# Feed-forward products by one level of Strassen's identity, the second product taken one Strassen product at a time

## The chip, the cores and the metric

The kernel runs on one core of a Trainium2 chip. The metric is the device time of one execution in microseconds (us). The kernel before takes 3463.45 us (median of three runs, 3463.38 to 3473.92). The engines of the core are named as in the profile: PE is the matrix engine (TensorE), DVE VectorE, ACT ScalarE, POOL GpSimd, and SP is the engine whose queue issues every DMA of this kernel.

## The reference, cut to what matters

One post-norm block over 2048 tokens of width 1024: a mixer of two head groups (a state-space group and an RWKV-7 group), an output projection, a layer norm, and then a feed-forward layer with an inner width of 4096 and a last layer norm. Only the feed-forward layer is touched.

```python
D_MODEL = 1024; SEQ = 2048; D_FF = 4 * D_MODEL
def sq_relu_mlp(h, w_fc, w_proj):
    return jnp.square(jax.nn.relu(h @ w_fc)) @ w_proj
...
h = layer_norm(ALPHA * h + mix, ln1_g[l], ln1_b[l])
h = layer_norm(ALPHA * h + sq_relu_mlp(h, w_fc[l], w_proj[l]), ln2_g[l], ln2_b[l])
```

All tensors are float32. The two products are 2048 x 1024 x 4096 ("up") and 2048 x 4096 x 1024 ("down").

## The kernel before, in words

Three phases follow one another: `phase_in` (layer norm, input projection), `phase_rwkv` (both head groups, with the output projection woven in as the pieces of a generator `k.fill`), and `phase_mlp` (the last pieces of `k.fill`, then the feed-forward layer). The tile framework orders the instructions of each engine by a timeline of its own; each engine then works off its list strictly in order, and waits where an operand or a buffer is not ready.

Every matrix product is made in three matmuls. An operand x is split into a high part that the matrix engine's float32r format holds and the rest, `hi` and `lo` (a cast on ACT, a subtraction on DVE or POOL), and the product is hi·hi + lo·hi + hi·lo. One matmul has a 128x128 stationary operand and a 128x512 moving one, and adds into one PSUM bank (128x512 float32).

`phase_mlp` takes the tokens in two blocks of 1024 (`blocks`: the eight middle token tiles first, since they leave the mixer first). For a block the transposed activations stand split in SBUF (`k.hh`, `k.hl`: eight transposes per token tile in PE, line 234, an ACT cast, line 235, a DVE subtraction, line 236). A loop over 16 groups (`NG`) of two 128-wide slices of the inner layer then does, for each slice, `weights` (two 512 KB loads, two casts, two subtractions, lines 1337 to 1349), `up` (2 x 24 matmuls, lines 1360 to 1362, and per 512 tokens a relu, a square, a cast and a subtraction, lines 1364 to 1367), and for the group before it `down` (lines 1380 to 1382, 12 matmuls per 128 tokens x 512 columns, added to an SBUF accumulator by DVE, line 1386). So up and down alternate through the whole phase and nothing goes back to DRAM. `down` of the last group is 24 matmuls per token tile and ends with the layer norm (`ln_apply`) and the store of that tile. `ln_apply` does its two passes over the row in DVE (lines 1306, 1308), or, with `spread`, one in ACT (line 1297) and two in POOL (line 1304).

PSUM has eight banks: `k.ps` has 4 (up, and the output projection's rest), `k.ps2` 4 (down, transposes).

## Time and profile before

| | |
|---|---|
| median of three runs | 3463.45 us |
| time of the profiled execution | 3468.34 us |
| its span, first to last instruction | 3466.6 us |
| mean granted clock of PE over the span | 0.931 |
| PE busy / DVE / ACT / POOL | 91% / 57% / 36% / 31% |
| feed-forward, first up matmul to last down matmul begun | 2033.07 to 3452.22 us |
| matmuls of the feed-forward | 3072 up and 3072 down |

A row of the groups reads: line, engine, operation, output<-inputs, shapes, count, then busy time, mean of one in ns, and the idle time of the engine just before, with what ended it. A row of the timeline reads: start, duration, engine, line, operation, and in brackets the idle time before with its releaser. A row of the windows gives, for a stretch of time, each engine's busy time and instruction count, PE's granted clock, the mean busy share of the 16 DMA engines and what they moved. Matmuls are pipelined: one is shown as busy for some 390 ns, while the next begins sooner.

### The profile page before, as it was taken

The page shows a single profiled execution, that of the slowest core. Times are in us where ns is not written, and L with a number is a line of the kernel's source. Part 1 is how long each engine was busy: PE and PEld are TensorE (multiplying, and loading weights), DVE is VectorE, ACT ScalarE, POOL GpSimd, SP SyncE. Part 2 cuts the span into 40 slices and gives each one's busy share as a digit, 9 for nine tenths or more (in the row PEclk, how much of TensorE's full clock was granted, in tenths as well). Part 3 has the DMA queues.
Part 4 walks back from the last instruction along what each step waited for, and adds up shares of the span by engine and source line. Part 5 has one row for each costly group of instructions (what it writes and reads, how often), then busy time and mean ns, then how long its engine had stood idle before and what let it go on. Part 6 is the DMA issues. An engine that isn't in the chain of part 4 may idle for free.

```text
span 3466.6 us, 62908 instructions
## 1 busy us (share of the span) xinstructions
PE 3166.2 (91%) x24551; PEld 2528.8 (73%) x24551; DVE 1971.3 (57%) x3722; ACT 1238.0 (36%) x2574; POOL 1058.1 (31%) x1742
## 2 busy tenths in 40 slices
PE   5879999988876798999889799999999999999998
PEld 4767867766665576777667578888888788888886
DVE  7798456777674555555766554444444654444446
ACT  3556323433335445455656431222122212222221
POOL 0352134444554333335565551111111111111113
PEclk9989999999985889886988899999999999999999
DMA  5345356776777566667665552111111331111111
GB/s 209 131 161 178 120 150 182 217 217 191 216 220 194 152 160 169 156 155 192 172 168 156 154 185 96 46 48 49 49 46 46 104 109 49 49 49 49 49 49 61
DMA packets 630137, 446.70 MB, mean 129 GB/s; under 512 B 193456, under 2 KB 553552, under 8 KB 629840
## 3 DMA queue, kind: packets, MB, share of 16 engines
q1 hardware_dynamic: 629840, 442.69, 43.7%
q8 instruction: 193, 3.16, 0.4%
q14 instruction: 104, 0.85, 0.1%
HBM read 295.43 MB, written 147.14 MB: 128 GB/s over the span
## 4 chain that ended last, share of the span: by engine, by line
PE 57%; DMA 15%; DVE 11%; issue 4%; POOL 4%; ACT 2%; SPq 2%; POOLq 0%; DVEq 0%; ACTq 0%
PE ps L1360 7%; PE ps L1362 7%; PE ps L1361 7%; PE ps L1382 6%; PE ps L1380 6%; PE ps L1381 6%; DMA R<-rows 2%; PE psg L266 2%; PE psg L267 2%; PE psg L268 2%; PE psg L826 2%; DMA la<-ad 2%; DMA ad<-at 2%; PE ch L1138 2%; DMA nd<-ln 1%
## 5 line engine op out<-in xcount | busy, mean ns | idle before, releaser
L1386 DVE TENSOR_TENSOR acc<-acc,ps 128x512 f32<-128x512 f32 x464 | 318.2, 687 | 445.5 <-PE ps L1382 443.2
L1367 POOL TENSOR_TENSOR ul<-r,uh 128x512 fp32r<-128x512 f32 x128 | 171.4, 1340 | 1186.9 <-ACT uh L1366 1186.9
L1362 PE MATMUL ps<-hl,fh 128*128 128x512 f32 x1024 | 401.8, 392 | 0.0
L1361 PE MATMUL ps<-hh,fl 128*128 128x512 f32 x1024 | 401.2, 392 | 0.0
L1360 PE MATMUL ps<-hh,fh 128*128 128x512 f32 x1024 | 397.7, 393 | 3.4 <-DVE h L831 3.1
L1382 PE MATMUL ps<-ph,ul 128*128 128x512 f32 x1008 | 393.3, 390 | 0.0
L1381 PE MATMUL ps<-pl,uh 128*128 128x512 f32 x1008 | 393.0, 390 | 0.0
L1380 PE MATMUL ps<-ph,uh 128*128 128x512 f32 x1008 | 392.8, 390 | 0.0
L266 PE MATMUL psg<-hh,wh 128*128 128x512 f32 x864 | 356.5, 413 | 9.9 <-ACT u L285 9.1
L267 PE MATMUL psg<-hh,wl 128*128 128x512 f32 x864 | 354.4, 410 | 0.0
L268 PE MATMUL psg<-hl,wh 128*128 128x512 f32 x864 | 352.1, 408 | 1.4 <-DVE hl L236 1.4
L1348 ACT CAST ph<-wraw 128x1024 fp32r<-128x1024 f32 x63 | 63.3, 1050 | 533.8 <-PE ps L1382 528.2
L1360 PEld LDWEIGHTS ps<-hh,fh 128*128 128x128 f32 x1024 | 192.2, 188 | 46.4 <-issue 3.5
L1361 PEld LDWEIGHTS ps<-hh,fl 128*128 128x128 f32 x1024 | 192.3, 188 | 42.7
L1362 PEld LDWEIGHTS ps<-hl,fh 128*128 128x128 f32 x1024 | 192.2, 188 | 42.8
L1382 PEld LDWEIGHTS ps<-ph,ul 128*128 128x128 f32 x1008 | 189.4, 188 | 40.7
L1381 PEld LDWEIGHTS ps<-pl,uh 128*128 128x128 f32 x1008 | 189.2, 188 | 40.8
L1380 PEld LDWEIGHTS ps<-ph,uh 128*128 128x128 f32 x1008 | 189.2, 188 | 40.7
L266 PEld LDWEIGHTS psg<-hh,wh 128*128 128x128 f32 x864 | 169.2, 196 | 49.5 <-ACT u L285 10.3
L1053 POOL TENSOR_TENSOR ltmp<-ln,la 128x30 f32<-128x30 f32 (+10 forms) x480 | 121.6, 254 | 248.7 <-DMA la<-ad 218.5
L268 PEld LDWEIGHTS psg<-hl,wh 128*128 128x128 f32 x864 | 168.2, 195 | 39.2 <-issue 3.0
L267 PEld LDWEIGHTS psg<-hh,wl 128*128 128x128 f32 x864 | 169.1, 196 | 35.7 <-issue 2.3
(291 smaller groups left out, 6148.5 us busy)
## 6 DMA issues: line engine op xcount, KB each, us to landing
h<-hD SPq DMA_DIRECT2D x64, 512.0 KB, 3.6
wraw<-in_w_fc_dram SPq DMA_DIRECT2D x64, 512.0 KB, 4.0
wraw<-in_w_proj_dram SPq DMA_DIRECT2D x64, 512.0 KB, 4.3
rk<-rk SPq DMA_DIRECT2D x64, 384.0 KB, 4.7
eD<-et SPq DMA_DIRECT2D x32, 514.0 KB, 2.7
E<-eD SPq DMA_DIRECT2D x64, 257.0 KB, 4.7
xs<-xg SPq DMA_DIRECT2D x64, 256.0 KB, 4.1
R<-rows SPq DMA_DIRECT2D x64, 256.0 KB, 4.4
```

What stands on the lines that cost most here:

```text
L266: nc.tensor.matmul(pt, wh[:, c], hh[:, c], start=(c == 0), stop=False)
L267: nc.tensor.matmul(pt, wl[:, c], hh[:, c], start=False, stop=False)
L268: nc.tensor.matmul(pt, wh[:, c], hl[:, c], start=False, stop=(c == KC - 1))
L1053: eng.tensor_tensor(tv, ln[:, 0:m, r:r + 1].broadcast_to([P, m, w]), la[:, r:r + 1, r + 1:16].broadcast_to([P, m, w]), ALU.mult)
L1360: nc.tensor.matmul(pt, wh[:, c], k.hh[:, c, ns], start=(c == 0), stop=False)
L1361: nc.tensor.matmul(pt, wl[:, c], k.hh[:, c, ns], start=False, stop=False)
L1362: nc.tensor.matmul(pt, wh[:, c], k.hl[:, c, ns], start=False, stop=(c == KC - 1))
L1367: nc.gpsimd.tensor_tensor(ul[:, ns], r, uh[:, ns], ALU.subtract)
L1380: nc.tensor.matmul(pt, uh[:, ts], ph[:, hs], start=(i == 0), stop=False)
L1381: nc.tensor.matmul(pt, uh[:, ts], pl[:, hs], start=False, stop=False)
L1382: nc.tensor.matmul(pt, ul[:, ts], ph[:, hs], start=False, stop=(i == len(ops) - 1))
L1386: nc.vector.tensor_tensor(acc[j][:, hs], acc[j][:, hs], pt, ALU.add)
```

## The change

Both products go by one level of Strassen's identity (in Winograd's form): each operand is cut into 2 x 2 quarters, seven products of sums of quarters replace eight of quarters.

- **Up.** A step is a token block (1024) and a pair of 128-wide slices (16 pairs, `NP`). Each of the seven products has 12 matmuls into a bank of 512 tokens; products 2 and 3 add into the banks of 1 and 5. Sums of the weight quarters are made by POOL (`sums_a`, 4 operations per step), those of the activations once per block (`hprep`, `sums_b`: on DVE for the first block, on POOL, through DRAM `hT`, for the second). Seven splits of weight sums per step (ACT cast, DVE subtraction). The sums that give the four quarters of the inner activations are made from the banks (`post`: one copy in ACT, five additions in DVE), then relu and square in ACT.
- **Between.** The inner activations do not stay in SBUF. DVE makes the seven left operands of down from their quarters (`sums_a`, 4 operations per step), unsplit, and seven stores per step put them into DRAM (`uD`). The right operands of down are made from `w_proj` in 16 of the 32 steps (`pprep`: 4 loads, 4 POOL sums, 7 stores to `pD`).
- **Down.** It starts after the last step of up. Per block it takes one product after the other (`DOWN`), each over all eight groups of the inner layer; the four 128-token tiles of a product stand in four banks. A step (block, product, group) loads 512 KB of `uD` and 512 KB of `pD`, splits both (two casts in ACT, one subtraction in DVE, one in POOL), three steps ahead, and has 24 matmuls. After a product's eighth group `take` adds the four banks to the right quarters of `y` (the residual, loaded and scaled by ACT at the block's first product); the last two products end with the layer norm and the store.
- **Banks and buffers.** `k.ps` has 6 banks, `k.ps2` 2. The weight tiles `wa`, `wh`, `wl` and the scratch `sc` have one buffer each; the down operands four.

The diff's core:

```diff
+ORDER = (1, 6, 7, 5, 2, 4, 3)
+DOWN = (1, 6, 7, 5, 2, 3, 4)
+def sums_a(eng, a, new):
+    for i in (5, 6, 3):
+        a[i] = new(i)
+    eng.tensor_tensor(a[5], a[7], a[4], ALU.add)
+    eng.tensor_tensor(a[6], a[5], a[1], ALU.subtract)
+    eng.tensor_tensor(a[7], a[1], a[7], ALU.subtract)
+    eng.tensor_tensor(a[3], a[2], a[6], ALU.subtract)
...
+        def hprep(b, i):
+            s = {}
+            for t, slots in ((blocks[b][i], (1, 2)), (blocks[b][4 + i], (7, 3))):
+                h = xp.tile([P, D], F32, name="h", bufs=2)
+                nc.sync.dma_start(h, k.hD[t])
+                for q in range(2):
...
+                    s[slots[q]] = scratch(slots[q])
+                    nc.scalar.copy(s[slots[q]], pt.rearrange("p j t -> p (j t)"))
+            sums_b(nc.gpsimd if b else nc.vector, s, scratch)
+            ts = slice(P * i, P * i + P)
+            for j in ORDER:
+                x = s[j].rearrange("p (c t) -> p c t", c=4)
+                if b:
+                    nc.sync.dma_start(hD[j][:, :, ts], x)
+                else:
+                    split(hh[j][:, :, ts], hl[j][:, :, ts], x)
...
+                mm = [(x[:, n], y[:, n]) for n in range(4) for x, y in ((hi, hh[i]), (lo, hh[i]), (hi, hl[i]))]
+                for n, (x, y) in enumerate(mm):
+                    nc.tensor.matmul(pt, x, y, start=(n == 0 and i not in (2, 3)), stop=(n == 11 and i not in (1, 5)), skip_group_check=True)
+                post(i, pt)
+                after(i)
+                between(i)
+            sums_a(nc.vector, c, lambda i: wp.tile([P, 512], F32, name=f"ua{i}"))
+            for i in ORDER:
+                nc.sync.dma_start(uD[b][q // 2][:, i - 1, q % 2], c[i])
...
+            for src, eng, names in ((uD[b][g], nc.vector, ("uh", "ul")), (pD[g], nc.gpsimd, ("ph", "pl"))):
+                hi, lo = (wk.tile([P, 2, 512], F32R, name=n) for n in names)
+                x = lo.bitcast(F32)
+                nc.sync.dma_start(x, src[:, i - 1])
+                nc.scalar.copy(hi, x)
+                eng.tensor_tensor(lo, x, hi, ALU.subtract)
...
+            for j in range(4):
+                ts = slice(P * j, P * j + P)
+                mm = [(x[:, r, ts], z[:, r]) for r in range(2) for x, z in ((uh, ph), (uh, pl), (ul, ph))]
+                for s, (x, z) in enumerate(mm):
+                    nc.tensor.matmul(banks[j], x, z, start=(g == 0 and s == 0), stop=(g == NG - 1 and s == 5))
+                if g == NG - 1:
+                    take(b, i, j, banks[j])
...
-        k.ps = pool("psumo", 4)
-        k.ps2 = pool("psumo2", 4)
+        k.ps = pool("psumo", 6)
+        k.ps2 = pool("psumo2", 2)
```

The order that the framework makes of it, at three places. In the rows a tile's name is followed by a number of its buffer; `cst` is the identity, `h` a token tile, `woh`, `yh` and the like belong to the output projection, and a wait names the engine or the DMA queue slot that it is for.

**Where up begins, PE.** Before, the last matmul of the output projection is followed by the first of up:

```order
L826 MATMUL ps_24135<-wol_17121,yh_24055 128x512
L826 MATMUL ps_24135<-woh_17120,yl_24057 128x512
L1360 MATMUL ps_24213<-hh_23763,fh_23770 128x512 [waits DMAHW3_49,DMAHW4_49,DMAHW2_49,DMAHW5_49,DMAHW0_49,DVE_49]
L1361 MATMUL ps_24213<-hh_23763,fl_23772 128x512
L1362 MATMUL ps_24213<-hl_23764,fh_23770 128x512
```

Now (L1381 are the transposes of `hprep`, L1495 the matmuls of up, `hh1` and `wh1` the high parts for product 1, `hh6` and `wh6` for product 6):

```order
L826 MATMUL ps_24301<-woh_17120,yl_24239 128x512
L1381 MATMUL ps2_24003<-cst_60,h_24001 128x128 [waits DMAHW0_49,Activation_49]
L1381 MATMUL ps2_24019<-cst_60,h_24017 128x128 [waits DMAHW2_49,Activation_49]
L1381 MATMUL ps2_24111<-cst_60,h_24109 128x128 [waits DMAHW3_49,Activation_49]
L1381 MATMUL ps2_24127<-cst_60,h_24125 128x128 [waits DMAHW4_49,Activation_49]
L1381 MATMUL ps2_24717<-cst_60,h_24715 128x128 [waits DMAHW0_49,Activation_49]
L1495 MATMUL ps_24381<-hh1_23801,wh1_24338 128x512 [waits DVE_49,Activation_49]
L1495 MATMUL ps_24400<-hh6_23803,wh6_24342 128x512 [waits DVE_49,Activation_49]
L1495 MATMUL ps_24381<-hh1_23801,wl1_24339 128x512 [waits DVE_49]
```

The transposes of the third and fourth pair of token tiles of the first block have moved behind the whole output projection, and the second matmul of up belongs to product 6 and waits for that product's weights.

**The first weights, SP and then POOL, now** (`sc` are the scratch tiles that `hprep` uses too, so a load into one waits until DVE has made the last split out of it; L1304 is the layer norm of the last token tile):

```order
L1436 DMA sc1_24217<-in_w_fc_dram 128x4x128 [waits DVE_49]
L1376 DMA h_25284<-hD1_83 128x1024 [waits DMAHW0_49,PE_49]
L1436 DMA sc2_24223<-in_w_fc_dram 128x4x128 [waits DVE_49,Activation_49]
L1436 DMA sc7_24219<-in_w_fc_dram 128x4x128 [waits DVE_49]
L1436 DMA sc4_24221<-in_w_fc_dram 128x4x128 [waits DMAHW6_49,DVE_49]
L836 DMA hD15_97<-h_24232 128x1024 [waits Activation_49,Pool_49]
```

```order
L1330 TENSOR_TENSOR sc5_24225<-sc7_24219,sc4_24221 128x512 [waits DMAHW6_49,DMAHW5_49,DVE_49]
L1304 TENSOR_TENSOR h_24232<-h_24232,b1_17620 128x512 [waits Pool_49]
L1304 TENSOR_TENSOR h_24232<-h_24232,rsb_17622 128x256 [waits Pool_49]
L1304 TENSOR_TENSOR h_24232<-h_24232,rsb_17624 128x256
L1331 TENSOR_TENSOR sc6_24226<-sc5_24225,sc1_24217 128x512 [waits DMAHW2_49,DVE_49,Pool_49]
L1332 TENSOR_TENSOR sc7_24219<-sc1_24217,sc7_24219 128x512 [waits DVE_49]
```

The sum `sc6` that product 6 needs stands behind `sc5` and three operations of a layer norm.

**Where down begins, SP now** (`ua1`, `ua2` and `ua4` are operands that the last step of up stores, `ul` and `pl` the tiles that the loads of down fill, `y` the residual):

```order
L1501 DMA uD1_7_23775<-ua1_30206 128x512 [waits DMAHW2_49,Activation_49]
L1501 DMA uD1_7_23775<-ua2_30222 128x512 [waits DMAHW3_49,Activation_49]
L1539 DMA ul_30265<-uD0_0_23760 128x1024 [waits DMAHW4_49,PE_49]
L1539 DMA pl_30270<-pD0_23776 128x1024 [waits DMAHW5_49,PE_49]
L1539 DMA ul_30275<-uD0_1_23761 128x1024 [waits DMAHW6_49]
```

and, four steps of loads later, the residual of both blocks, eight token tiles ahead of the loads of step 5 and seven ahead of those of step 6:

```order
L1539 DMA ul_30361<-uD0_4_23764 128x1024 [waits DMAHW1_49,DVE_49,PE_49]
L1315 DMA row_g_30294<-in_ln2_g_dram 128x1024 [waits DMAHW2_49]
L1552 DMA y_30298<-hD4_86 128x1024 [waits DMAHW4_49]
L1552 DMA y_30319<-hD11_93 128x1024 [waits DMAHW3_49]
L1539 DMA ul_30395<-uD0_5_23765 128x1024 [waits DMAHW4_49,DVE_49,PE_49]
L1539 DMA pl_30400<-pD5_23781 128x1024 [waits DMAHW5_49,Pool_49]
L1552 DMA y_32414<-hD0_82 128x1024 [waits DMAHW6_49]
L1552 DMA y_32432<-hD14_96 128x1024 [waits DMAHW4_49]
L1539 DMA ul_30429<-uD0_6_23766 128x1024 [waits DMAHW5_49,DVE_49,PE_49]
```

Before, loads of `w_fc` and `w_proj` alternate through the whole phase; now the first loads of down stand behind a store that waits for the last step of up.

More of the change, by code (lines that the diff above doesn't have):

```diff
@@ L1402, in phase_mlp, with wtile, wraw @@
                     break
+        def wtile(i):
+            return wp.tile([P, 512], F32, name=f"wa{i}")
+        def wraw(q, new=wtile):
+            a = {}
+            for i, hf, f in ((1, 0, 0), (7, 0, 1), (4, 1, 1), (2, 1, 0)):
+                a[i] = new(i)
+                c0 = P * (2 * q + f)
+                nc.sync.dma_start(a[i].rearrange("p (c m) -> p c m", c=4),
+                                  I["w_fc"][512 * hf:512 * hf + 512, c0:c0 + P].rearrange("(c p) m -> p c m", p=P))
+            sums_a(nc.gpsimd, a, new)
+            return a
@@ L1403, in phase_mlp @@
+        a = wraw(0, scratch)
         for _ in k.fill:
             pass
-        cp = ctx.enter_context(tc.tile_pool(name="mlp_c", bufs=1))
-        wk = ctx.enter_context(tc.tile_pool(name="mlp_w", bufs=2))
-        rows = load_rows(k, cp, ("ln2_g", "ln2_b"))
-        for bi, toks in enumerate(blocks):
-            acc = []
-            prev = None
-            for gi in range(NG):
-                ops = [up(first.pop() if first else weights(G * gi + i, bi and G * gi + i == DFF // P - 1)) for i in range(G)]
-                if bi == 0 and gi == NG - 1:
-                    operands()
-                    for j, t in enumerate(blocks[1]):
-                        transpose_split(k, load(t), k.hh, k.hl, P * j)
-                if prev and not (bi and gi == NG - 1):
-                    down(toks, acc, prev, gi == 1)
-                    prev = []
-                prev = (prev or []) + ops
-            down(toks, acc, prev, False, rows)
+        wp = ctx.enter_context(tc.tile_pool(name="mlp_w", bufs=1, reuse_waits="tile"))
@@ new lines, in phase_mlp, with after, between @@
+        w = {i: wsplit(a, i) for i in ORDER}
+        steps = [(b, q) for b in range(2) for q in range(NP)]
+        pslots = [(0, q) for q in (3, 6, 9, 12)] + [(1, q) for q in range(1, 13)]
+        for n, (b, q) in enumerate(steps):
+            a = wraw(steps[n + 1][1]) if n + 1 < len(steps) else None
+            nw = {}
+            def after(i):
+                if a:
+                    nw[i] = wsplit(a, i)
+            def between(i):
+                if b == 0 and q == NP - 1:
+                    hload(i)
+            if b == 0 and q in (2, 5, 8, 11):
+                hprep(1, (q - 2) // 3)
+            if (b, q) in pslots:
+                m = pslots.index((b, q))
+                pprep(m // 2, m % 2)
+            if (b, q) == (0, NP - 2):
+                hahead()
+            up(b, q, w, after, between)
+            w = nw
```

214 lines of the change are left out of this document (145 added, 69 removed).

## The prediction

> **What bounds the kernel now.** I read the page first, then the windows of the feed-forward, then its groups. Page: the span, PE's clock and the DMA rate in 40 slices of 87 us, and the chain of waits.
>
> ```profile
> span 3466.6 us, 62908 instructions
> PEclk9989999999985889886988899999999999999999
> GB/s 209 131 161 178 120 150 182 217 217 191 216 220 194 152 160 169 156 155 192 172 168 156 154 185 96 46 48 49 49 46 46 104 109 49 49 49 49 49 49 61
> PE 57%; DMA 15%; DVE 11%; issue 4%; POOL 4%; ACT 2%; SPq 2%; POOLq 0%; DVEq 0%; ACTq 0%
> ```
>
> From slice 24 on the clock is full and DMA almost idle. Windows (length; busy time and count for PE, PEld, DVE, ACT, POOL; clock; DMA share; GB/s):
>
> ```profile
> 2000.00:2033.00 33.00, 30.25 (x130) 23.81 (x128) 20.84 (x35) 14.17 (x21) 21.08 (x19) 0.95 0.78 263
> 2900.00:3100.00 200.00, 200.00 (x875) 164.05 (x874) 84.00 (x109) 42.58 (x57) 23.29 (x18) 1.00 0.17 53
> 3453.00:3467.00 14.00, 0.00 (x0) 0.00 (x0) 9.05 (x12) 1.83 (x3) 5.54 (x2) 0.58 0.22 89
> ```
>
> The feed-forward is a solid stream of matmuls: 200.00 us / 875 = 0.2286 us each, DVE 42% busy, ACT 21%, POOL 12%. Begin and end of the stream, and what follows it, from the timeline (start, duration):
>
> ```profile
> 2033.07 0.50 PE L1360 MATMUL ps<-hh,fh 128*128 128x512 f32 x1
> 3452.22 0.39 PE L1382 MATMUL ps<-fh,ul 128*128 128x512 f32 x1
> 3459.48 3.17 DVE L1308 SCALAR_TENSOR_TENSOR acc<-acc,ln_rs,row_b 128x1024 f32<-128x1024 f32 x1
> ```
>
> 6144 x 0.2286 = 1404.5 of the 1419.5 us between 2033.07 and 3452.6; nearly all the rest is the second block's transposes (64, 8.9 us busy). So a matmul taken out is worth its 0.2286 us, as long as nothing else paces PE; and everything that makes PE pause is paid in full.
>
> **The sum: what is removed.** Up: 2 blocks x 16 pairs x 7 products x 12 = 2688 matmuls; down: 2 x 7 x 8 x 24 = 2688. 5376 in place of 6144, all of the shape of before: 768 x 0.2286 = **-175.5 us**.
>
> **What the other engines get.** Their prices, from the groups of the feed-forward:
>
> ```profile
> L1386 DVE TENSOR_TENSOR acc<-acc,ps 128x512 f32<-128x512 f32 x464 | 318.2, 687 | 445.5 <-PE ps L1382 443.2
> L1365 DVE TENSOR_TENSOR r<-r 128x512 f32<-128x512 f32 x126 | 88.3, 700 | 116.1 <-ACT r L1364 114.9
> L1366 ACT CAST uh<-r 128x512 fp32r<-128x512 f32 x127 | 78.9, 621 | 108.0 <-DVE r L1365 108.0
> L1367 POOL TENSOR_TENSOR ul<-r,uh 128x512 fp32r<-128x512 f32 x128 | 171.4, 1340 | 1186.9 <-ACT uh L1366 1186.9
> L1349 DVE TENSOR_TENSOR pl<-wraw,ph 128x1024 fp32r<-128x1024 f32 x60 | 70.9, 1223 | 0.1
> L1348 ACT CAST ph<-wraw 128x1024 fp32r<-128x1024 f32 x60 | 60.1, 1049 | 528.2 <-PE ps L1382 528.2
> L1304 POOL TENSOR_TENSOR acc<-acc,row_b 128x1024 f32<-128x1024 f32 x4 | 13.0, 3244 | 0.3
> L1304 POOL TENSOR_TENSOR acc<-acc,row_g 128x1024 f32<-128x1024 f32 x4 | 9.5, 2382 | 22.6 <-ACT acc L1297 22.6
> L236 DVE TENSOR_TENSOR hl<-ps,hh 128x512 fp32r<-128x512 f32 x16 | 10.1, 686 | 8.1 <-ACT hh L235 7.9
> L235 ACT CAST hh<-ps 128x512 fp32r<-128x512 f32 x16 | 8.7, 610 | 7.6 <-PE ps L234 4.6 <-PE ps L1361 3.0
> ```
>
> A step of up lasts 84 x 0.2286 = 19.2 us on PE. DVE has 16 operations of 128x512 (7 splits, 5 bank additions, 4 sums): 16 x 0.70 = 11.2. ACT 16 x 0.62 = 9.9. POOL 4 x 1.34 = 5.4, or 10.7 with the sums of `pprep` or `hprep`. Weights are loaded and split a whole step ahead, and a bank is wanted again three products (8.2 us) after its release at the earliest, so I cost the steady steps at nothing. That cover is PE's 19.2 us; if DVE or DMA exceeds it, the excess comes in every step. A step of down is 24 x 0.2286 = 5.5 us: ACT 2 x 1.05 = 2.1, DVE 1.2, POOL about 2.4. Free too, with loads three steps (16.5 us) ahead.
>
> Then the pauses.
>
> *Entry, +32 (16 to 45).* Up starts when the first block is split and summed. Before that took 16 DVE operations, now 4 pairs x (7 splits + 4 sums) = 44, and ACT 4 x (4 + 7) = 44 casts and copies, in the stretch where the output projection's last rows and their layer norms run:
>
> ```profile
> 1998.25 0.50 PE L826 MATMUL ps<-woh,yh 128*128 128x512 f32 x1 [0.64 <-ACT sd L1216]
> 2002.39 0.69 DVE L217 BATCH_NORM_STATS2 ln_st<-h 128x6 f32<-128x512 f32 x1
> 2009.97 1.29 POOL L1304 TENSOR_TENSOR h<-h,gl 128x512 f32<-128x512 f32 x1
> h<-hD SPq DMA_DIRECT2D x64, 512.0 KB, 3.6
> ```
>
> The order puts the first transposes behind the second of the five remaining token rows, and their loads behind stores of the mixer, so about 2008 to 2010. From there DVE has 44 x 0.69 = 30.4, and for three rows 6 additions and 6 statistics, 8.3, with small ones 41 us; with 5 for taking turns with ACT (none to 15) that ends near 2055. Only then may the last scratch tile be loaded with weights: 3 us (512 KB take 3.6), `sc5` 1.3, three pieces of layer norm 2.7, `sc6` 1.3, cast 0.6: 9 us. PE's second matmul waits for it: 2064, and 2065 with a slow clock (below), against 2033. DVE at 41 us without turns and the weights in time would make it 2049.
>
> *Change of block, +3 (0 to 10).* Seven operand pairs are reloaded in two steps; each has six products (16.5 us) from its last use to its next, and costs 1 MB, a cast of 2.1 us and a subtraction of 2.5 in DVE or 5.1 in POOL. The rest is room.
>
> *Up to down, +9 (6 to 15).* The first load stands behind the store of `ua2`, about 0.7 us before the last matmul of up. Load 4, second load 0.4 later, two casts 2.1: PE idles about 5.6; then four matmuls, and POOL's subtraction (2.4) is short by 1.6. A slow clock adds 2.
>
> *Residual, +13 (5 to 22).* 16 token tiles (8.4 MB) and two rows (1 MB) are queued among the loads of steps 4 to 7. The rate that a full DMA reaches, from slices of 0.8 us in 2000 to 2033 (busy tenths, GB/s):
>
> ```profile
> DMA  9999425678023039999959877999899999957799
> GB/s 377 408 390 408 170 94 168 168 214 238 12 68 91 0 81 257 354 416 374 430 194 199 327 222 202 278 350 369 353 328 377 384 357 342 271 121 288 293 184 367
> ```
>
> At 370 GB/s step 4's buffer comes free when step 0 ends; from there 7.3 MB until step 5 has its data, 20 us, plus 2 to land, two casts and POOL's 2.4: 26.5 against 22 us of matmuls: 4 late. Step 6, 4.7 MB more, 13 us against 5.5: 7 late. Clock 2. At 430 GB/s it is 7 and at 300 GB/s 19, both without the clock.
>
> *Rest of down, +5 (0 to 12).* Product 7 ends with eight POOL additions (10.7 us) among its subtractions, the last two products with two layer norms in POOL (2.4 + 3.2 each). Room is 6 to 7 us, so a microsecond or two each, in five places.
>
> *Tail, +11 (4 to 14).* Before, the end is 14.0 us after the last matmul (3452.6). Now four tiles end within 4.1 us. DVE: 4 additions, 8 statistics, small ones and three passes of 1.3 to 1.9 until the last `spread` scale is known, 13.5 us from 4.1 before the end of PE; ACT 1.2; four POOL passes 2 x 2.4 + 2 x 2.4 to 3.2; and the store 3.9 (3459.48 + 3.17 to 3466.6): about 25.
>
> *The clock* is in these terms. After an idle PE it is half for a while:
>
> ```profile
> 2020.92 0.50 PE L826 MATMUL ps<-woh,yl 128*128 128x512 f32 x1 [2.17 <-POOL yl L815]
> 2022.18 0.63 PE L826 MATMUL ps<-woh,yh 128*128 128x512 f32 x1
> 2022.60 0.63 PE L826 MATMUL ps<-wol,yh 128*128 128x512 f32 x1
> ```
>
> 0.42 us apart in place of 0.23 for some 2.5 us, 1.2 us lost; idle times of 4 to 30 us are longer, so I take 2 per pause. The Trainium skill (TensorE: Matmul & The Clock Gate, Part 1) says that an idle window of about 3.4 us halves the clock, and a busy one of 3.4 restores it: by it 1.7 per window, an estimate, and four pauses would cost 7 where I have about 8. The trace agrees.
>
> Sum: -175.5 + 32 + 3 + 9 + 13 + 5 + 11 = -102.5. The profiled execution took 3468.34 (span 3466.6), so by it **3365.8**. It lies 4.9 above the median of the three runs, 3463.45; for the median I say 3361.
>
> **Rivals.**
>
> *Up is paced by DVE (slower than I think, still faster than before).* DVE and POOL disturb each other:
>
> ```profile
> 2016.38 2.27 POOL L1304 TENSOR_TENSOR h<-h,b 128x512 f32<-128x512 f32 x1
> 2017.43 2.31 DVE L1349 TENSOR_TENSOR pl<-wraw,ph 128x1024 fp32r<-128x1024 f32 x1
> 1988.19 0.69 DVE L236 TENSOR_TENSOR hl<-ps,hh 128x512 fp32r<-128x512 f32 x1 [0.16 <-ACT hh L235]
> ```
>
> 2.31 in place of 1.22, 2.27 in place of 1.28. 11 of DVE's 16 operations read two SBUF tiles; all slowed 1.9 times they take 14.6, with the 5 others 18.1, with 0.16 before each 20.7: 1.5 over 19.2, 32 steps: +48, 3409. Against it: POOL is at work only 5.4 to 10.7 of 19.2 us. The Trainium skill (GPSIMD Engine Reference, section 1, Specifications) says that POOL shares its SBUF interfaces with VectorE, with contention where VectorE has two SBUF inputs. The trace agrees; it names the sums and splits that this change adds.
>
> *Up is paced by DMA: slower than before.* A step with `pprep` or `hprep` (20 of 32) moves 1.05 + 1.84 + 1.05 + 1.84 = 5.8 MB, 300 GB/s at 19.2 us. No slice of the page has more than 220. At 220 the step takes 26.3: 20 x 7.1 = +142, 3503. It decides from 5.1 us per step on, 5.8 / 24.3 = 238 GB/s. For it: in-order SP, some 22 issues per step, many of which wait. Against it: 263 GB/s at a share of 0.78 in the window above, and slices up to 430.
>
> *The pauses are small.* All low bounds: -175.5 + 31 = -144.5: 3319.
>
> *Nothing is gained*, since a short wait in every step (32 of up, 112 of down) takes what 768 matmuls gave: 102 / 144 = 0.7 us per step, near 3463. The stream of before shows no such wait with the same kind of buffers (200.00 of 200 us busy).
>
> **How the numbers follow.** Forecast 0.70 (own range 3330 to 3400), DVE-paced 0.13, DMA-paced 0.09, small pauses 0.05, no gain 0.03. Predicted 3361. Range 3325 to 3420: it takes in DVE's pace and most of the small pauses, and leaves out the rest. Within 0.3% of 3463 a measurement hardly tells from no change. Faster 0.88, same 0.03, slower 0.09.
>
> **What would show it.** Windows inside up and inside down: some 437 matmuls per 100 us at clock 1.00, DVE below 70% in up, DMA share 0.4 to 0.8; PE idle in four places: before the first L1495 (to about 2064), before the first L1599 (6 us), within the first product of down behind DMA `y`, and at the end (25 us after the last matmul). Fewer than 420 matmuls per 100 us in up says a rival is right: DVE near 95%, or loads of `wa` that land late at a DMA share of 0.9. First up matmul before 2050 or after 2080 makes the entry wrong.

## The result, and the profile after

The changed kernel takes 3368.77 us (median of four runs, 3359.39 to 3376.91) against 3468.68 us of the kernel before in the same comparison (median of four). One of those four executions of the kernel before took 3622.25 us, far above the other three (3463.38 to 3473.92); without it the changed kernel takes 0.9716 of the time before, with a 95% interval of 0.9678 to 0.9754. The profiled execution of the change took 3370.11, with a span of 3368.3, so 98.3 us less span than before; forecast were 102.5.

The page: span, granted clock and DMA rate in 40 slices (84 us each now).

```profile
span 3368.3 us, 63962 instructions
PEclk9989999989896788898798987999999989999998
GB/s 205 135 158 183 123 147 174 204 213 197 207 216 243 134 160 158 160 156 179 170 187 158 154 152 150 236 251 235 258 326 306 141 296 194 193 214 210 189 197 152
```

DMA is no longer idle from slice 25 on, and two slices of up carry over 300 GB/s. The windows (length; busy time and count for PE, PEld, DVE, ACT, POOL; clock; DMA share; GB/s): inside the first block of up, the change of block, the second block with `pprep` in every step, the first product of down, the middle of down.

```profile
2110.00:2300.00 190.00, 189.63 (x864) 157.00 (x864) 144.16 (x154) 95.32 (x167) 105.11 (x66) 1.00 0.71 238
2380.00:2430.00 50.00, 40.89 (x168) 32.40 (x167) 42.08 (x34) 26.08 (x36) 35.76 (x16) 0.93 0.85 307
2480.00:2580.00 100.00, 95.98 (x416) 78.61 (x415) 76.58 (x79) 43.86 (x78) 70.61 (x47) 0.98 0.95 322
2720.00:2765.00 45.00, 39.02 (x152) 30.52 (x151) 11.24 (x6) 30.91 (x30) 18.14 (x8) 0.89 1.00 386
3100.00:3300.00 200.00, 200.00 (x884) 165.62 (x883) 95.62 (x62) 77.19 (x74) 109.67 (x49) 1.00 0.58 193
```

In the first PE hardly waits and in the last not at all, as forecast. In the last, 884 matmuls fall into 200 us, 0.2262 us each, where before it was 0.2286. In the three between PE waits, and its clock sags. DVE is at 76% in up, not below 70%.

The places where PE waits, from its timeline (start, duration, idle time before with what ended it). In order: the first two matmuls of up, the change of block, `pprep` in the second block, the last matmul of up, the begin of down, its steps 5 and 6, the end of product 7, the last matmul.

```profile
2063.63 0.80 PE L1495 MATMUL ps<-hh,wh 128*128 128x512 f32 x1 [5.11 <-ACT wh L1358]
2071.80 0.79 PE L1495 MATMUL ps<-hh,wh 128*128 128x512 f32 x1 [7.38 <-ACT wh L1358]
2415.21 0.80 PE L1495 MATMUL ps<-hh,wh 128*128 128x512 f32 x1 [5.99 <-ACT ux L1469]
2572.54 0.50 PE L1495 MATMUL ps<-hh,wh 128*128 128x512 f32 x1 [3.78 <-DVE ua L1480]
2710.08 0.39 PE L1495 MATMUL ps<-hl,wh 128*128 128x512 f32 x1
2716.49 2.08 PE L1599 MATMUL ps<-ph,uh 128*128 128x512 f32 x4 [6.03 <-ACT ph L1540]
2750.14 0.50 PE L1599 MATMUL ps<-pl,uh 128*128 128x512 f32 x1 [1.26 <-POOL pl L1541]
2759.20 2.07 PE L1599 MATMUL ps<-ph,uh 128*128 128x512 f32 x4 [4.22 <-ACT ph L1540]
3065.45 0.79 PE L1599 MATMUL ps<-pl,uh 128*128 128x512 f32 x1 [2.83 <-POOL pl L1541]
3346.47 0.39 PE L1599 MATMUL ps<-ph,ul 128*128 128x512 f32 x1
```

Behind a long wait the granted clock is half (0.50) for a while. The window of the begin of down, whose 14 matmuls take 0.43 us each:

```profile
2716.50:2723.20 6.70, 6.33 (x14) 4.55 (x15) 4.54 (x2) 4.18 (x4) 5.92 (x3) 0.50 1.01 363
```

From these rows the 98.2 us divide as follows. The matmuls: 6144 x 0.2286 before, 5376 x 0.2262 now, -188.4. The entry: the third matmul of up starts at 2072.39, which is 38.9 later than with nothing to wait for after 2033.07. Up: 637.9 from there to its end at 2710.31, of which 2686 matmuls are 607.6, so 30.3 of pauses and transposes, against 15.0 in the whole stream before, +15.3. Up to down +6.2. Down: 630.4 from 2716.49 to 3346.9, of which matmuls 608.0, +22.4. The tail: 21.4 against 14.0, +7.4. The pauses are 90.2 together. The 38.9 of the entry are counted from the time at which up began before, 2033.07. Counted from the last matmul of the output projection they are 42.9, since in this execution that matmul starts at 2028.53, and at 2032.56 in the kernel before. How much of these 4.0 us is the change, which puts 40 transposes behind the projection, and how much is the mixer, which varies from execution to execution, was not separated.

DVE and POOL at work together, in a step of up that has `pprep` (first DVE, then POOL; L1330 to L1333 on DVE are the sums of `ua`, L1472 and L1480 read a bank; L1340 to L1343 on POOL are the sums of `pprep`):

```profile
2131.35 0.69 DVE L1480 TENSOR_TENSOR ua<-u,ps 128x512 f32<-128x512 f32 x1 [1.33 <-PE ps L1495]
2134.49 1.67 DVE L1331 TENSOR_TENSOR ua<-ua,ua 128x512 f32<-128x512 f32 x1
2136.08 1.77 DVE L1332 TENSOR_TENSOR ua<-ua,ua 128x512 f32<-128x512 f32 x1
2137.78 1.77 DVE L1333 TENSOR_TENSOR ua<-ua,ua 128x512 f32<-128x512 f32 x1
2141.17 0.68 DVE L1472 TENSOR_TENSOR u<-ux,ps 128x512 f32<-128x512 f32 x1
...
2133.98 1.63 POOL L1341 TENSOR_TENSOR sc<-sc,sc 128x512 f32<-128x512 f32 x1
2135.57 1.73 POOL L1342 TENSOR_TENSOR sc<-sc,sc 128x512 f32<-128x512 f32 x1
2137.27 1.74 POOL L1343 TENSOR_TENSOR sc<-sc,sc 128x512 f32<-128x512 f32 x1
```

An operation of DVE with two SBUF inputs takes 1.7 to 1.8 us beside POOL's; one with a PSUM input takes 0.67 to 0.69 at any time (all 159 of them in up). At the change of block, where POOL has a 128x2048 subtraction, one small DVE sum takes as long as that:

```profile
2401.08 5.09 DVE L1330 TENSOR_TENSOR ua<-ua,ua 128x512 f32<-128x512 f32 x1
2399.72 5.90 POOL L1418 TENSOR_TENSOR hl<-hl,hh 128x2048 fp32r<-128x2048 f32 x1 [2.52 <-ACT hh L1417]
```

So the theory to test is: the pauses of up and of the entry, which came out longer than forecast, are DVE waiting for POOL. Its rival is the DMA (322 GB/s at a share of 0.95 in the second block), and for the entry and down the queues and the order of the work. The tail is shorter than forecast, but the same question is asked of it.

### The profile page after: what moved, and what is told of

It is laid out like the page before. It is cut to its first block, busy times and chain, and to the rows that moved or that the text cites. A ratio compares the mean times of both kernels' runs of the same rounds, so it can differ in the third digit from the quotient of the medians.

```text
span 3368.3 us, 63962 instructions
## 1 busy us (share of the span) xinstructions
PE 3003.0 (89%) x23783; PEld 2397.6 (71%) x23783; DVE 2167.9 (64%) x3675; ACT 1536.7 (46%) x2993; POOL 1570.1 (47%) x1968
## 5 line engine op out<-in xcount | busy, mean ns | idle before, releaser
L1541 DVE TENSOR_TENSOR ul<-ul,uh 128x1024 fp32r<-128x1024 f32 x112 | 245.2, 2189 | 290.4 <-ACT uh L1540 290.1
L1541 POOL TENSOR_TENSOR pl<-pl,ph 128x1024 fp32r<-128x1024 f32 x112 | 287.0, 2567 | 281.6 <-ACT ph L1540 281.6
L1495 PE MATMUL ps<-hh,wh 128*128 128x512 f32 x896 | 352.5, 394 | 25.8 <-ACT wh L1358 12.9
L1495 PE MATMUL ps<-hl,wh 128*128 128x512 f32 x896 | 350.5, 391 | 1.5 <-DVE hl L1418 1.4
L1495 PE MATMUL ps<-hh,wl 128*128 128x512 f32 x896 | 350.4, 391 | 0.0
L1359 DVE TENSOR_TENSOR wl<-wa,wh 128x512 fp32r<-128x512 f32 x217 | 209.7, 971 | 85.2 <-ACT wh L1358 84.2
L1540 ACT CAST ph<-pl 128x1024 fp32r<-128x1024 f32 x112 | 117.7, 1051 | 288.2 <-DMA pl<-pD 288.2
L1358 ACT CAST wh<-wa 128x512 fp32r<-128x512 f32 x217 | 132.9, 618 | 207.0 <-POOL wa L1331 98.4
L1495 PEld LDWEIGHTS ps<-hh,wh 128*128 128x128 f32 x896 | 169.6, 189 | 65.0 <-ACT wh L1358 14.2
L1495 PEld LDWEIGHTS ps<-hl,wh 128*128 128x128 f32 x896 | 169.2, 189 | 37.9 <-DVE hl L1418 1.8
```

What stands on the lines that cost most here:

```text
L1358: nc.scalar.copy(hi, x)
L1359: nc.vector.tensor_tensor(lo, x, hi, ALU.subtract)
L1495: nc.tensor.matmul(pt, x, y, start=(n == 0 and i not in (2, 3)), stop=(n == 11 and i not in (1, 5)), skip_group_check=True)
L1540: nc.scalar.copy(hi, x)
L1541: eng.tensor_tensor(lo, x, hi, ALU.subtract)
```

## The experiments

The start of up differs by up to 25 us between executions of kernels with the same entry, since the mixer ahead of it does. So the kernels are compared by the lengths of their stages in the profiled execution: **entry**, from the last matmul of the output projection to the third of up; **up**, from there to its last matmul; **first product**, from the first matmul of down to the first copy out of its first product; **down**, from its first matmul to its last; **tail**, from there to the end of the span. Each of the eight kernels with a single edit was executed once, the four combined ones four times. All times are in us.

| kernel | entry | up | first product | down | tail |
|---|---|---|---|---|---|
| the change | 43.9 | 637.7 | 53.5 | 630.0 | 21.8 |
| extra_stores | 43.9 | 636.2 | 54.1 | 629.2 | 21.8 |
| even_pprep | 43.9 | 632.0 | 54.8 | 629.9 | 21.8 |
| weight_sums_dve | 42.3 | 625.8 | 51.0 | 624.1 | 21.8 |
| no_residual | 43.9 | 637.6 | 48.4 | 624.4 | 21.8 |
| paced_residual | 43.9 | 638.4 | 44.7 | 623.1 | 21.8 |
| hload_dve | 43.9 | 628.8 | 54.4 | 627.1 | 21.8 |
| tail_one_spread | 43.9 | 637.4 | 53.7 | 628.9 | 19.0 |
| early_first_weights | 39.6 | 646.3 | 50.2 | 623.2 | 21.8 |
| together | 39.6 | 625.6 | 45.1 | 623.4 | 18.9 |
| together_pl_dve | 39.6 | 630.2 | 43.8 | 612.5 | 18.9 |
| entry_ln_dve | 30.2 | 625.0 | 43.0 | 612.5 | 18.9 |
| up_sums_dve | 33.1 | 617.7 | 41.7 | 610.9 | 18.9 |

(The expectations have 40.2, 625.0 and 629.6 in places where the table has 39.6, 625.6 and 630.2: in these kernels the timeline joins the first two matmuls of up in one row, and the fourth was taken for the third.)

A stage that an edit does not touch repeats within 0.1 us in entry and tail. In up it repeats within 1.0 in four kernels (637.4 to 638.4), but once it moved by 4.6 (`together` against `together_pl_dve`), so a difference of up below some 5 us between two kernels proves little by itself. In down it varies from 627.1 to 630.0. In `weight_sums_dve` and `early_first_weights` the framework ordered the residual's loads otherwise (four or six tiles ahead of the loads of step 6 in place of seven), and their first product is shorter; that the order is the reason was not tested.

### Is it the DMA? More traffic

```diff
                 nc.sync.dma_start(pD[g][:, i - 1, r], s[i])
+                nc.sync.dma_start(pX[g][:, i - 1, r], s[i])
```

> Each of the seven sums of `pprep` is stored a second time, into a DRAM tensor that nothing reads: 1.84 MB more in each of the 16 steps with `pprep`, 7.7 MB per step in place of 5.8, and no work for an engine but seven issues on SP. If DMA has the reserve that single slices show (430 GB/s), 7.7 MB in 19.2 us (400 GB/s) still fit: up ends within 5 us of the 2710 us of the changed kernel. If the 322 GB/s at a share of 0.945 of the stretch 2480 to 2580 are nearly the ceiling (340 at a share of 1), a step takes 22.6 to 23.9 us, 3.4 to 4.7 more in the twelve steps that follow one another: up ends 41 to 56 us later, and PE's waits there end with weights that land late.

Two windows of the second block, and the issues of `pprep`'s loads between 2420 and 2650:

```profile
2470.00:2570.00 100.00, 100.00 (x443) 82.78 (x442) 73.21 (x87) 49.80 (x87) 52.78 (x36) 1.00 0.94 328
2420.00:2650.00 230.00, 227.72 (x1004) 187.91 (x1002) 172.08 (x198) 112.69 (x195) 124.44 (x83) 1.00 0.95 335
sc<-in_w_proj_dram SPq DMA_DIRECT2D x35, 256.0 KB, 4.4
```

The longer window in the change:

```profile
2420.00:2650.00 230.00, 225.50 (x984) 185.25 (x983) 179.09 (x193) 107.73 (x189) 137.41 (x90) 0.99 0.83 281
```

Up is 1.5 us shorter, not 41 to 56 longer: DMA is busier over the 230 us (a share of 0.95 against 0.83), and PE waits less, so DMA does not pace up. But the reserve is not what the other side expected either: where the change already had 322 GB/s, the rate rose only to 328, at the same share. What gave way is `pprep`. In a stretch as long the change issues 40 of its loads, this kernel 35: the extra stores delay `pprep`, for whose results PE waits only in down. The traffic that up itself needs is 2.9 MB per step. And since POOL's sums are now fewer per step (36 operations in 100 us against 47), the wait of 3.8 us before 2572.5 is gone, which points at POOL.

### Is it where `pprep` stands?

```diff
-        pslots = [(0, q) for q in (3, 6, 9, 12)] + [(1, q) for q in range(1, 13)]
+        pslots = [(0, q) for q in (1, 3, 4, 6, 7, 9, 10, 12)] + [(1, q) for q in (2, 4, 6, 8, 10, 12, 13, 14)]
```

> The 16 steps with `pprep` are spread over both blocks (steps 1, 3, 4, 6, 7, 9, 10, 12 of the first and 2, 4, 6, 8, 10, 12, 13, 14 of the second) in place of four in the first and twelve in a row in the second. If DMA is what holds up the second block (two neighbouring steps then move 8.7 MB in 38.4 us, 227 GB/s), the wait of 4.2 us before 2572.5 and the steps of 20.6 to 21.8 us go, all steps without transposes take 19.0 to 19.3, and up ends 5 to 7 us earlier, near 2704. If it is POOL's sums of `pprep`, which slow DVE's operations, a step with `pprep` takes 20 to 22 us wherever it stands, and up ends near 2710 as before.

Up got 5.7 us shorter, as the first answer said, and the second block's steps from its third on take 18.6 to 20.2 us in place of up to 21.8 (from one copy of ACT into `ux` to the next, of which each step has one). The second answer, that a step with `pprep` takes 20 to 22 us wherever it stands, did not come: with eight of them in the first block its 15 steps take 296.1 us, against 294.9 with four. So the work of `pprep` costs PE little where its steps are spread. That alone does not tell DMA from POOL, because both are thinned out; the run before and the next one do.

### Is it POOL beside DVE?

```diff
-            sums_a(nc.gpsimd, a, new)
+            sums_a(nc.vector, a, new)
```

> The four sums of the weight quarters of each step go from POOL to DVE, 20 DVE operations per step in place of 16. If DVE's operations with two SBUF inputs are long (1.0 to 1.8 us against 0.68 with a PSUM input) because POOL works at the same time, they fall to about 0.70 in the steps where POOL now has nothing, DVE is busy some 14 us per step as before although it does more, and up ends within 4 us of 2710. If they are long for a cause of their own, DVE is busy 18 to 20 us per step, paces it, and up ends 15 to 40 us later.

Windows of this kernel in the first and second block, and its group of weight splits (2110 to 2300), with the same group of the change behind it:

```profile
2110.00:2300.00 190.00, 190.00 (x869) 157.91 (x868) 140.59 (x197) 97.48 (x168) 42.27 (x27) 1.00 0.73 241
2425.00:2655.00 230.00, 229.51 (x1013) 189.73 (x1012) 184.68 (x254) 114.15 (x198) 63.16 (x40) 1.00 0.83 285
L1359 DVE TENSOR_TENSOR wl<-wa,wh 128x512 fp32r<-128x512 f32 x68 | 50.7, 746 | 19.3 <-ACT wh L1358 19.3
```

```profile
L1359 DVE TENSOR_TENSOR wl<-wa,wh 128x512 fp32r<-128x512 f32 x67 | 66.7, 995 | 25.5 <-ACT wh L1358 25.4
```

DVE makes 197 operations in 190 us in place of 154 and is busy for less time, 140.6 in place of 144.2. Up is 11.9 us shorter, more than I had expected, with the same DMA traffic (285 GB/s against 283 in 2425 to 2655). So DVE's operations are long because of POOL. Of the 11.9, some 7 are at the change of block: the three steps around it take 61.1 us in place of 68.4. The Trainium skill (SBUF — State Buffer, Who interferes with whom) says that a DVE instruction with two SBUF inputs contends with a GpSimd instruction that reads SBUF, that this contention is an exclusive lock, and that a DVE instruction with at most one SBUF input, outside the 2-port perf modes, does not contend. The trace agrees: the DVE sum of 5.09 us ended 0.5 us after POOL's subtraction, and DVE's additions from a bank stay at 0.68.

### The change of block

```diff
-            (nc.gpsimd if j in (5, 4) else nc.vector).tensor_tensor(hl[j], lo, hh[j], ALU.subtract)
+            nc.vector.tensor_tensor(hl[j], lo, hh[j], ALU.subtract)
```

> At the change of block the two 128x2048 subtractions of `hload` that POOL makes (4.6 and 5.9 us) go to DVE (2.3 us each), which then makes all seven. If DVE's sum that took 5.1 us (at 2401.1) was held by POOL's long subtraction, it falls to 0.7 to 1.8, the wait of 6.4 us before 2415.2 falls to under 2, and up from its third matmul to its last takes 4 to 7 us less than 637.7. If DVE is simply the late engine there, 4.6 us more on it make the wait longer: up takes 0 to 4 us more.

The same DVE sum in this kernel:

```profile
2383.64 0.68 DVE L1330 TENSOR_TENSOR ua<-ua,ua 128x512 f32<-128x512 f32 x1
```

0.68 in place of 5.09. PE's longest wait at the change of block is now 1.7 us, and up is 8.8 shorter; I had expected 4 to 7. More work on DVE shortened the stage.

### The residual

Left out:

```diff
-                nc.sync.dma_start(y[t], k.hD[t])
-                nc.scalar.mul(y[t], y[t], ALPHA)
+                nc.scalar.mul(y[t], rows[0][0], ALPHA)
```

> The 16 loads of the residual (8.4 MB) are left out: `y` is made from the row of the layer norm's gain instead, so the last layer norm works on other numbers. If the loads of steps 5 and 6 are late because of the residual, the waits between 2747 and 2762 (2.2, 4.4 and 1.6 us, with a slow clock after them) go, and down, from its first matmul at 2716.5 to its last at 3346.5, takes 8 to 11 us less than 630.0. If they come from the start of the pipeline itself (three loads ahead, POOL's first subtractions), they stay and it takes at most 3 us less.

Loaded one tile at a time:

```diff
-                y[t] = ap_.tile([P, D], F32, name="y", bufs=NT)
-                nc.sync.dma_start(y[t], k.hD[t])
-                nc.scalar.mul(y[t], y[t], ALPHA)
+                y[t] = ap_.tile([P, D], F32, name="y", bufs=8)
+                raw = ap_.tile([P, D], F32, name="raw")
+                nc.sync.dma_start(raw, k.hD[t])
+                nc.scalar.mul(y[t], raw, ALPHA)
```

> The residual is loaded into one tile `raw` with a single buffer and scaled from there into `y` (eight buffers in place of sixteen), so that each of its loads waits for the scaling of the one before, and the second block's for the first block's stores. If the mass of residual loads in the queue (8.4 MB at once) is what made steps 5 and 6 late, down falls from 630.0 us to the 624.4 of the kernel without the residual, or below, since ACT's scalings are spread too. If SP, which works in order, is held at each of these waits (load 3.5 and scaling 1.1 us) and holds the loads of the next steps behind it, down takes 633 us or more, and the waits stand at steps 4 to 8.

ACT without the loads, just ahead of step 5:

```profile
2725.22 15.27 ACT L1552 ACTIVATE y<-row_g 128x1024 f32<-128x1024 f32 x16 [0.91 <-DMA row_g<-in_ln_g_dram]
```

Without the loads the first product took 5.1 us less and down 5.6, between the two answers: a wait of 2.7 us for ACT's cast at step 5 stayed. All sixteen scalings now run at once in ACT, 15.27 us ahead of the casts, so this kernel leaves out the loads and gathers the scalings. Paced, the first product took 8.8 us less and down 6.9, and no wait is left in it after its first four matmuls. So 8.8 us is the price of the residual as the change loads it, by the loads and by ACT's scalings in a burst; how much is which was not measured. About 2 us came back at the end of product 7:

```profile
3050.84 0.80 PE L1600 MATMUL ps<-pl,uh 128*128 128x512 f32 x1 [5.30 <-POOL pl L1541]
```

This wait is 2.83 in the change. No wait shows that SP, held at the waits of these loads, did harm.

### The tail

```diff
-                finish(t2, j % 2 == 1)
+                finish(t2, j == 0 if b else j % 2 == 1)
```

> In the very last product only the first of the four token tiles has its layer norm spread over ACT and POOL; the other three stay in DVE. Now the end comes 21.8 us after the start of the last matmul, with POOL's four passes of 2.3 us begun only 9 us after it. If POOL's passes set the end, the first tile's two passes start some 3 us after the last matmul and DVE, with 2.5 us more, ends near 13: the end comes 15 to 18 us after the last matmul. If DVE's passes set it, or its operations slow by POOL's at the same time, the end stays at 21 to 23.

2.9 us shorter, a little less than expected. POOL's passes in the tail of the change, and then DVE's in the tail of this kernel:

```profile
3355.42 4.64 POOL L1304 TENSOR_TENSOR y<-y,row_g 128x1024 f32<-128x1024 f32 x2 [16.22 <-ACT y L1297]
3360.01 4.63 POOL L1304 TENSOR_TENSOR y<-y,row_b 128x1024 f32<-128x1024 f32 x2
```

```profile
3357.91 4.54 DVE L1306 SCALAR_TENSOR_TENSOR y<-y,ln_mv,row_g 128x1024 f32<-128x1024 f32 x2
3362.58 3.15 DVE L1308 SCALAR_TENSOR_TENSOR y<-y,ln_rs,row_b 128x1024 f32<-128x1024 f32 x1
3365.66 1.27 DVE L1306 SCALAR_TENSOR_TENSOR y<-y,ln_mv,row_g 128x1024 f32<-128x1024 f32 x1
```

In the change DVE's passes take 1.2 to 1.3 us and are over before POOL's begin; POOL's four passes (9.2 us) and the store behind them (3.7) end the kernel. In this kernel, where DVE has passes left beside POOL's (3358.83 to 3364.65), a pass takes 1.27 alone and up to 3.2 beside them. So POOL set the end of the change, as the first answer said, and DVE beside POOL took back a part of the gain.

### The entry

```diff
-        a = wraw(0, scratch)
+        ht = [xp.tile([P, D], F32, name="h", bufs=2) for _ in range(2)]
+        raw = {1: ht[0][:, :512], 7: ht[0][:, 512:], 4: ht[1][:, :512], 2: ht[1][:, 512:]}
+        a = wraw(0, lambda i: raw[i] if i in raw else scratch({5: 1, 6: 6, 3: 7}[i]))
```

> The raw weights of the first step go into the two `h` tiles, which are free after the last transposes, in place of four scratch tiles, and their sums into the three scratch tiles that are split first. Now the third matmul of up starts 43.9 us after the last one of the output projection. If the wait is a chain behind DVE's last split (load, POOL's sums between pieces of the layer norm, cast: 10 us), it falls to 34 to 38 us, and DVE's splits set it. If the sums are late because POOL has the layer norm of the last rows first, or DVE's splits slow by as much as POOL's sums now overlap with them, it stays at 42 or more.

The entry fell to 39.6, not to 34 to 38, and the gain was lost again: up is 8.6 us longer. The next cast of weights, for product 7, waits for the store of the last row of the output projection, and PE for that cast:

```profile
2075.37 0.62 ACT L1358 CAST wh<-h 128x512 fp32r<-128x512 f32 x1 [7.93 <-DMA hD<-h]
2076.04 0.80 PE L1497 MATMUL ps<-hh,wh 128*128 128x512 f32 x1 [3.26 <-ACT wh L1358]
```

The tile `wh7` lies where that row lay. So behind the chain of the weights stands a second one, the layer norm and the store of the last row, which ended at 2073 in the change too, hidden by the first.

### Together

The edits above in one kernel (sums of the first step stay on POOL), and the tiles that up needs late given out first, so that `wh7` lies elsewhere:

```diff
         wp = ctx.enter_context(tc.tile_pool(name="mlp_w", bufs=1, reuse_waits="tile"))
+        for n_ in ("ux", "u1", "u2", *(f"ua{i}" for i in range(1, 8))):
+            wp.tile([P, 512], F32, name=n_)
+        for i in range(1, 8):
+            wtile(i)
...
-            sums_a(nc.gpsimd, a, new)
+            sums_a(nc.vector if new is wtile else nc.gpsimd, a, new)
```

> Together: the weight sums of every step but the first on DVE, `pprep` spread evenly, all of `hload` in DVE, the paced residual, one spread tile at the end, the early first weights, and with these the tiles of `mlp_w` that up needs late (`ux`, `u1`, `u2`, `ua`, `wa`) given out first, so that the first split weights no longer lie where the last row of the mixer's layer norm still is. Each did by itself: sums on DVE 637.7 to 625.8 us of up, residual 630.0 to 623.1 of down, tail 21.8 to 18.9; entry 43.9 to 40.2, lost again by a wait of 3.7 for the store of that last row. If these are separate places and that wait is one of memory, they add up: -12, -7, -3, -4, some 26 us less than 3368.8, near 3343. If DVE, with 20 to 22 operations per step, now sets the pace, or the late wait comes from the layer norm itself and not from its memory, up takes 630 or more and the entry stays at 43: 3355 or more.

3337.40 us against 3457.92 before in the same comparison, 0.9651 (0.9624 to 0.9679). Entry -4.3, up -12.1, down -6.6, tail -2.9, which add up to the 26 expected; in the profiled execution the output projection also ended 6.9 us earlier than in that of the change. The wait for the store is gone with the place in memory. In up the edits do not add: the weight sums alone gave 11.9, `pprep` spread evenly 5.7 and the subtractions at the change of block 8.8, and all three together 12.1, which fits three edits that reach the same waits.

The same, and both subtractions of down in DVE:

```diff
-            for src, eng, names in ((uD[b][g], nc.vector, ("uh", "ul")), (pD[g], nc.gpsimd, ("ph", "pl"))):
+            for src, eng, names in ((uD[b][g], nc.vector, ("uh", "ul")), (pD[g], nc.vector, ("ph", "pl"))):
```

> The same, and the subtraction of `pl` in down goes from POOL to DVE too, so that DVE makes two per step of 5.49 us. If `ul` and `pl` are long (2.19 and 2.57 us) because they run at the same time, each falls to 1.2 to 1.3, DVE is busy 2.5 us of a step as before, the wait for POOL's `pl` after product 7 (2.8 to 5.7 us) and the short ones after product changes go, and down takes 618 to 621 us, 2 to 5 less than in the kernel `together`. If DVE is late instead where it has the additions and the layer norms at the end of a product, waits of the same size stand there for DVE, and down takes as long or longer.

3329.91 us, 0.9624 (0.9605 to 0.9643). The subtractions of down, with those of the change (2770 to 3300) behind them:

```profile
L1547 DVE TENSOR_TENSOR ul<-ul,uh 128x1024 fp32r<-128x1024 f32 x111 | 144.7, 1303 | 15.3 <-ACT uh L1546 14.2
L1547 DVE TENSOR_TENSOR pl<-pl,ph 128x1024 fp32r<-128x1024 f32 x111 | 142.9, 1288 | 218.4 <-ACT ph L1546 217.8
```

```profile
L1541 DVE TENSOR_TENSOR ul<-ul,uh 128x1024 fp32r<-128x1024 f32 x97 | 213.2, 2198 | 248.5 <-ACT uh L1540 248.5
L1541 POOL TENSOR_TENSOR pl<-pl,ph 128x1024 fp32r<-128x1024 f32 x97 | 246.4, 2544 | 211.1 <-ACT ph L1540 211.1
```

Two subtractions in DVE take 2.6 us, hardly more than the one that it had (2.2) beside POOL's. Down is 10.9 us shorter than in `together`, more than the 2 to 5 expected: the wait after product 7 is gone (it was 5.3 there), and the slow clock after it. Up was 4.6 longer in the profiled execution, although nothing was changed there, with three waits of 1.7 to 3.5 us behind DVE's `ua` where `together` has one; the two medians differ by 7.5.

### POOL out of the entry, and out of up

The layer norm of the last five rows of the output projection in DVE:

```diff
-                ln_apply(k, wk, h, *rows, k.eps[:, 0:1], True)
+                ln_apply(k, wk, h, *rows, k.eps[:, 0:1], t not in (13, 1, 14, 0, 15))
```

> As `together_pl_dve`, and the layer norm of the last five rows of the output projection is made in DVE (two passes of 1.3 us per row in pieces) in place of ACT and POOL (five pieces, 6.5 to 8.3 us of POOL per row). Now the third matmul of up starts 39.6 to 40.2 us after the last one of the output projection, and in that stretch DVE's splits and sums take 1.2 to 1.8 us beside POOL's pieces and 0.68 without. If POOL's pieces are what stretches the entry, it gets 5 to 10 us shorter (30 to 35), though DVE has more to do. If DVE's number of operations sets it (28 splits, 16 sums), it gets longer by the 8 to 10 us of passes, 44 or more.

3318.31 us against 3465.28, 0.9592 (0.9559 to 0.9626). The splits of the entry in the change (2009 to 2062) and in this kernel (2003 to 2049):

```profile
L1359 DVE TENSOR_TENSOR hl<-sc,hh 128x512 fp32r<-128x512 f32 x28 | 24.5, 904 | 0.0
```

```profile
L1359 DVE TENSOR_TENSOR hl<-sc,hh 128x512 fp32r<-128x512 f32 x25 | 16.2, 674 | 0.0
```

The entry is 30.2, 9.4 us shorter, with more operations on DVE. So it was POOL's layer norm that stretched it; the shorter splits account for some 6.4 of the 9.4 (28 x 0.23), and where the rest comes from was not separated.

And the last of POOL's work in up given to DVE:

```diff
-            sums_b(nc.gpsimd if b else nc.vector, s, scratch)
+            sums_b(nc.vector, s, scratch)
...
-            sums_b(nc.gpsimd, s, scratch)
+            sums_b(nc.vector, s, scratch)
```

> As `entry_ln_dve`, and the sums of `pprep` and `hprep` go to DVE too, so that POOL has nothing to do in up, and DVE 24 operations per step where one of them stands. If every wait of up behind DVE's `ua` (3.9 us in one of the kernels before, 3.0, 2.1 and 3.9 in the other) comes from POOL beside it, all operations fall to 0.68, 24 of them take 16.3 of 19.0 us, and up takes 618 to 622 us from its third matmul to its last, against 625.0 and 629.6. If DVE is full before that (gaps for ACT's casts and the banks), it paces the steps with 24 operations: 20 us and more in 20 steps, 635 or more.

3308.64 us (3304.39 to 3312.44), 0.9551 of the kernel before (0.9530 to 0.9572), the best of all kernels here. The whole of up, and two of its groups (weight splits, a sum of weights):

```profile
2049.00:2667.00 618.00, 617.25 (x2750) 511.01 (x2748) 460.53 (x723) 318.50 (x531) 0.00 (x0) 1.00 0.73 250
L1359 DVE TENSOR_TENSOR wl<-wa,wh 128x512 fp32r<-128x512 f32 x217 | 148.0, 687 | 49.3 <-ACT wh L1358 49.3
L1331 DVE TENSOR_TENSOR wa<-wa,wa 128x512 f32<-128x512 f32 x31 | 21.3, 688 | 0.6
```

The same stretch of the change:

```profile
2072.50:2710.50 638.00, 623.21 (x2743) 512.36 (x2741) 480.09 (x515) 315.18 (x535) 333.05 (x207) 0.99 0.71 241
```

POOL makes nothing, DVE 723 operations where the change has 515 (2072.5 to 2710.5), and its busy time is 460.5 in place of 480.1. PE is busy for 617.25 of 618 us. Up takes 617.7, below what I had expected, and no wait behind `ua` is left. The entry is 2.9 longer than in the run before. There POOL's first sum of weights, which stays on POOL in both kernels, waited for DVE (first row); here it came in between DVE's operations (second row), and a DVE split beside the next sum took 1.75 us:

```profile
2045.90 6.41 POOL L1330 TENSOR_TENSOR sc<-h 128x512 f32<-128x512 f32 x1 [35.78 <-DMA h<-in_w_fc_dram]
2039.19 1.31 POOL L1330 TENSOR_TENSOR sc<-h 128x512 f32<-128x512 f32 x1 [35.40 <-DMA h<-in_w_fc_dram]
```

## Why the prediction was right, and where not

3361 was forecast and 3368.8 came, within its own range of 3330 to 3400. The time was right partly because two errors had opposite signs: the pauses are 17 us longer than forecast (90.2 against 73), the matmuls 12.9 us shorter. A part of the closeness may be luck in another way too: among the kernels here that share one entry, the output projection ahead of it ends anywhere from 2012.5 to 2038.0, more than the 7.8 us by which the forecast missed. The stages tell more than the total.

- **What is removed.** 5376 matmuls of the same shape: right. That they keep 0.2286 us each was wrong: they start 0.2262 apart, -188.4 in place of -175.5.
- **Steady steps at nothing.** Right for the first block: 15 steps, from ACT's first copy into `ux` to the sixteenth, in 294.9 us, that is 19.0 each and 9.9 for the transposes and one short wait. Not for the second: its steps with `pprep` and the waits there cost some 7 us. What failed is the price of DVE, "16 x 0.70 = 11.2", taken from rows in which POOL was mostly idle. Measured are 1.0 for a split and up to 1.78 for a sum beside POOL, and DVE at 75% where I said below 70%.
- **Entry, +32.** Measured 38.9. The order of the chain was right (DVE's splits, the load into the last scratch tile, POOL's sums among the layer norm, the cast: 2061.6 to 2071.8, 10 us against 9). The term that was too small is "44 x 0.69 = 30.4": the splits took 0.90 on average, and DVE ended at 2062 in place of 2055. `entry_ln_dve` shows why. Not foreseen was the second chain through the last row's memory.
- **Change of block, +3.** The mis-sized one. Up has 15.3 more pauses than the whole stream before, 11 of them in the three steps around the change (21.9, 21.1 and 25.4 us in place of 19.0). "The rest is room" counted each engine by itself; DVE was held by POOL's two subtractions, and `hload_dve` got 8.8 of it back.
- **Up to down, +9.** Right, at about 10: 6.2 of idle PE, then 0.4 after four matmuls (1.6 was forecast), and 14 matmuls at half the clock, which cost 3.3 and not 2.
- **Residual, +13.** The mechanism was right and steps 5 and 6 were the late ones; by `paced_residual` the price is 8.8. ACT's sixteen scalings in a burst belong to it, which the step did not name.
- **Rest of down, +5.** Down has 22.4 us of pauses; less the 8.8 and the 3.7 of the begin (0.4 and its slow clock), some 10 are left, where 5 were forecast. POOL's additions at the end of product 7 were named; that POOL's subtraction is 2.5 us and not 2.4 hardly matters, but DVE's 2.2 in place of 1.2 was not foreseen. Taking POOL out gave 10.9.
- **Tail, +11.** Measured 7.4. The chain was right (DVE, ACT's scale, four passes of POOL, the store), each piece a little shorter: POOL began 8.5 us after the last matmul, its passes took 9.2 and the store 3.7.
- **The clock, 2 per pause.** Too small. Behind six waits (2.8 to 7.4 us) some 29 us of matmuls ran at half the clock, which is some 14 us lost in place of about 8. That "the trace agrees" holds for the length of the slow stretch: in the kernel before the granted clock was 0.50 from 2021.7 to 2025.1, 3.4 us. But the idle time shown ahead of it is 2.17, so the rows do not show that 3.4 us of idle are needed.
- **The rivals.** *Up is paced by DVE* was the right mechanism at a quarter to two fifths of its price: DVE is stretched as described, but a step of 19.0 us absorbs most of it, and what reaches PE is 12 us by `weight_sums_dve` and 20 by `up_sums_dve`, not 48. *Up is paced by DMA* fell: 322 GB/s were asked for and granted in the second block, and with the extra stores, at 335 GB/s over 230 us, PE did not wait longer. Its "it decides from 238 GB/s" was wrong twice: the rate that DMA reaches is higher, and it counted `pprep`'s traffic as if PE waited for it. *The pauses are small* and *Nothing is gained* fell with the pauses as measured.

## What to carry to other kernels

Work given to POOL is not free because POOL is idle: where both it and DVE read two SBUF operands, count their times nearly as one sum. Here up, the entry and down were each shorter with such work on DVE, where an operation takes 0.68 us against POOL's 1.29. Before calling a stage bound by DMA, leave out the traffic that nothing in that stage waits for. And compare kernels by the lengths of stages in their traces, when the part ahead of the change varies by more than the change is worth.
